# Score products of a head pair made together in a one-core encoder step

## The chip, the cores and the metric

The kernel runs on one core of one Trainium2 chip. The metric is device time in microseconds (us), from three timed runs of the whole program; lower is better. TensorE (PE in the profile) multiplies matrices, VectorE (DVE) and ScalarE (ACT) work elementwise, GpSimd (POOL) helps them, and SyncE (SP) issues the DMA transfers.

## The reference, cut to what matters

One step of a hybrid encoder layer is computed for 512 prompt tokens and 8 x 16 sample tokens, in float32. Two groups of heads read the same normalised input:

```python
oa = band_attend(qa..., band_gather(ka, 8), band_gather(va, 8), valid, bias=bias)   # 16 heads, width 64
ob = band_attend(qb..., band_gather(kb, 2), band_gather(vb, 2), valid, sink=sinks)  # 16 query heads, 2 key heads
...
s = einsum(q, k) * 64 ** -0.5        # scores; bias added, invalid keys masked
p = exp(s - max); w = p / sum(p)     # group B adds a sink to max and sum
o = einsum(w, v)
```

Then follow an output projection, a gated feed-forward network and a last norm. The change touches only the prompt tokens' score products, `einsum(q, k)`, and the order in which heads are worked on.

## The kernel before, in words

Tokens lie on the free axis (512 prompt columns and 128 sample columns), features on the 128 partitions. Every float32 product is made of three passes over parts of reduced precision, high x high, low x high and high x low: `mm3` at L147 to L149. The input projections are the main stream on TensorE: `dense` makes one tile of 128 output features from 16 input tiles, with two halves of 320 tokens, 96 matmuls of 128x320 in all. They are called "dense matmuls" below; in the profile they write `dn`.

Attention is side work. It is written as generators whose `yield`s cut them into stages. After every 6 dense matmuls (one input tile) `dense` calls `pump`, which emits one more stage; `get` also calls it as long as no on-chip slot is free, and the drains call it until a queue is empty. Two streams take turns at first, `heads 0` and `heads 1`, each with a head of its own. From the fifth round of projections on (`p == 4`) `heads 1` gives its place to `decode`, the attention of the sample tokens. After the eight rounds `drain_queue("decode")` emits what is left of it.

A 128-row tile of queries holds two heads of width 64, one in rows 0 to 63, the other in rows 64 to 127. `scores` multiplies one head's 64 rows: for a block `i` of 128 queries it fills one PSUM bank with 128 to 512 columns (group A) or 128 and 256 columns (group B), and a DVE instruction (L323) adds bias or mask and takes the row's maximum. There are four such blocks to a head, emitted two to a stage. `softmax` is an ACT exponential for each block (L332) and a DVE scaling (L339). Then `flip` transposes the weights on TensorE (L248), and their products with the values end the head.

The banks of side work come from a pool of four (`at`). The framework's scheduler may set an instruction before or after its neighbours, so the order that stands in the program is told from the built program where it matters.

The named stretch is this:

Of the kernel before, what the change touches and what calls it, by code (L numbers as in the profile page):

```python
# [8 lines left out]
ALU = mybir.AluOpType  # L9
# [4 lines left out]
P = 128  # L14
# [4 lines left out]
SP = 512  # L19
# [14 lines left out]
def active(step):  # L34
    """Pairs of ff tiles on chip in a step of the second half: each stays for eight steps."""
    return [j for j in range(NPAIR) if (step - START[j]) % STEPS < 8]
# [13 lines left out]
class Net:  # L50
    """Emission helpers over a fixed set of on-chip slots handed out in program order."""

    def __init__(self, nc, tc, io, pools):
        self.nc, self.tc, self.io, self.pools = nc, tc, io, pools
        self.uid = 0
        self.lists = {"S": [f"S{i}" for i in range(N_S)], "W": [f"W{i}" for i in range(N_W)]}
        self.owner, self.turns = {}, {}
        self.queues, self.active, self.turn = {}, {}, 0
        self.streams = (("heads 0", "heads"), ("heads 1", "heads"))

# [11 lines left out]
    def pump(self):  # L72
        """Emit one more stage of the side work; streams take turns."""
        for _ in range(len(self.streams)):
            name, queue = self.streams[self.turn % len(self.streams)]
            self.turn += 1
            work = self.active.get(name)
            if work is None and self.queues.get(queue):
                work = self.active[name] = self.queues[queue].pop(0)
            if work is None or work.gi_running:  # L80
                continue
            try:
                next(work)
            except StopIteration:
                self.active[name] = None
            return True
        return False
# [23 lines left out]
    def keep_turns(self):  # L111
        """A slot's tiles take it in program order."""
        first = {}
# [45 lines left out]
    def dense(self, chunks, acts, outs=1):  # L159
        """One tile of outputs, or several that share the passes over acts."""  # L160
        ps = [self.banks() for _ in range(outs)]
        k = 0
        for i in range(0, len(chunks), outs):
            now = [c if len(c) == 3 else self.weights(*c) for c in chunks[i:i + outs]]
            for j in range(now[0][0]):
                ah, al = acts[k]
                for (_, w, _), out in zip(now, ps):
                    for a in range(2):
                        t = slice(a * HT, a * HT + HT)
# [7 lines left out]
    def rstd_steps(self, parts, dim, out):  # L177
        """1 / sqrt(mean + eps) of the tokens of each half, in all partitions."""
        nc = self.nc
        ps, n = self.bank(), len(parts)  # L180
# [48 lines left out]
def build(nc, tc, io, pools):  # L229
# [33 lines left out]

# [1 line left out]
    n.move("S", "C", 7)  # L265
# [5 lines left out]

# [1 line left out]
    START_CHUNKS = {0: (24, 0, 2, "S"), 1: (25, 0, 2, "S"), 2: (24, 2, 8, "WH"), 4: (25, 2, 8, "WH"),  # L273
# [42 lines left out]

# [1 line left out]
    def scores(q, k, rr, i, k0, k1, bias, s, mx):  # L318
        ps = n.bank()[:, :k1 - k0]
        rows = slice(64 * rr, 64 * rr + 64)  # L320
        qs, ks = slice(128 * i, 128 * i + 128), slice(k0, k1)
        n.mm3(ps, (q[0][rows, qs], q[1][rows, qs]), (k[0][rows, ks], k[1][rows, ks]), True, True)
        nc.vector.tensor_tensor_reduce(s, ps, bias, 1.0, -3e38, ALU.add, ALU.max, mx)  # L323

# [28 lines left out]

    def prompt_a(h, q, k, v, ot, done):
        rr = h % 2
        bias, t0, t1 = n.get("S"), n.get("S"), n.get("S")
        dma(out=bias[:, :SP], in_=io["bias_a"][h])
        yield
        es = [t0[:, 512:640], t1[:, :256], t1[:, 256:640], t0[:, :512]]
        mx = n.small(4)  # L360
        for pick in ((0, 3), (1, 2)):
            for i in pick:
                scores(q, k, rr, i, 0, P * (i + 1), bias[:, SP - P * (i + 1):SP], es[i], mx[:, i:i + 1])
            yield
        softmax(es, mx, None)
        n.put("S", bias)
        yield
        yield
        yield
        yield  # L370
        blk = lambda i, j: es[i][:, P * j:P * j + P]
# [7 lines left out]
        o2, p2 = flip([blk(i, 2) for i in range(2, 4)], "S")  # L379
        n.put("S", t0, t1)  # L380
        yield
# [7 lines left out]

    def prompt_b(t, rr, q, ot, done):  # L390
        sink = sinks[:, 8 * rr + t:8 * rr + t + 1]
        t0, t1 = n.get("S"), n.get("S")
        es = [t0[:, 512:640], t0[:, :256], t0[:, 256:512], t1[:, :256]]
        mx = n.small(4)
        for pick in ((0, 1), (2, 3)):
            for i in pick:
                k0 = max(0, i - 1) * P
                w = (i + 1) * P - k0
                scores(q, kb, rr, i, k0, k0 + w, mask_b[:, 256 - w:], es[i], mx[:, i:i + 1])
            yield  # L400
        softmax(es, mx, sink)
        yield
        yield
        yield
        yield
        oa, pa = flip([es[0], es[1][:, :P], es[2][:, P:], es[3][:, :P]], "S")
        yield
        ob, pb = flip([es[1][:, P:], es[2][:, :P], es[3][:, P:]], "S")
        n.put("S", t0, t1)
        yield  # L410
# [11 lines left out]
    def heads_of(kind, p, held, *args):  # L422
# [10 lines left out]

        for rr in range(2):
            n.add("heads", kind(*((2 * p + rr,) if kind is prompt_a else (p, rr)), *args, ot, done))

# [170 lines left out]

# [1 line left out]
    n.add("heads", input_norm())  # L609
# [46 lines left out]
    for p in range(8):  # L656
# [3 lines left out]
        if p == 4:  # L660
# [3 lines left out]
            n.put("D", cos, sin)  # L664
            while n.active.get("heads 1"):
                n.pump()
            n.streams = (("heads 0", "heads"), ("decode", "decode"))
# [3 lines left out]

# [1 line left out]
    n.put("S", *xg, r_mix)  # L673
# [37 lines left out]

# [1 line left out]
    more = group_operands(oa_d, g_a, ssq_a, range(4, 8))  # L713
    own_a, acts_a = own_a + more[0], acts_a + more[1]

    def prepare(kts, in_place=()):
        """The seven left operands of pairs of feature tiles, one product at a time."""
        work = []
# [49 lines left out]

# [1 line left out]
    n.move("WH", "H", 4)  # L770
# [3 lines left out]
    def quartet(k, load, lefts, before=None, after=None, part="all"):  # L774
        """Weights b11, b12, b21, b22 against the seven left operands; yields each
        product's name and bank. The late part has the two products that only add
        to the first half of the tokens."""

# [130 lines left out]

# [1 line left out]
    sums, waiting = [], []  # L911
# [63 lines left out]

# [1 line left out]
    r_y = n.get("S")  # L977
# [131 lines left out]
```

## Time and profile before

| | |
|---|---|
| median of the three timed runs | 2725.25 us (2723.32 to 2726.64) |
| profiled execution: span from first to last instruction | 2722.2 us |
| median of the runs less that span (what lies around it) | 3.05 us |
| PE busy | 2645.7 us (97%) |
| DVE, ACT, POOL busy | 1933.8, 1063.8, 787.2 us |
| mean granted TensorE clock | 0.988 of full speed |

Matmuls overlap in the profile: each is busy for about 0.3 us while the next one starts after 0.15 us. So the time that a matmul costs is read from the start of one to the start of the next, and a stretch's pace from the number of matmuls that start in it.

### The profile page before, as it was taken

How to read it: one execution, taken by the hardware profiler on the slowest of the kernel's cores; microseconds unless marked ns; L12 is line 12 of the kernel's file. 1: busy time of each engine (PE TensorE's matmuls, PEld its weight loads, DVE VectorE, ACT ScalarE, POOL GpSimd, SP SyncE). 2: the span in 40 equal slices, each digit the busy share in tenths (PEclk: the TensorE clock that was granted, in tenths of full speed). 3: DMA queues.
4: the chain of work that ended last, by engine and by line, in shares of the span. 5: the costliest groups of instructions: out<-in, count | busy, mean ns of one | idle time of the engine just before them, and what ended most of it. 6: DMA issues, size and time to landing. Idle time of an engine off the chain costs nothing.

```text
span 2722.2 us, 45156 instructions
## 1 busy us (share of the span) xinstructions
PE 2645.7 (97%) x17757; PEld 2584.7 (95%) x17757; DVE 1933.8 (71%) x2947; ACT 1063.8 (39%) x1718; POOL 787.2 (29%) x564
## 2 busy tenths in 40 slices
PE   7999999999999999999999999999999899999986
PEld 7999999899899999999999999999999899999986
DVE  6555565655666678776767667667677878888897
ACT  4333333433544454333333333333334444444443
POOL 3000000000212123333343333333434533444453
PEclk9999999999899999999999999999999999999998
DMA  5222223333556443333232333332334644444334
GB/s 163 86 77 76 82 75 100 108 117 113 165 182 214 148 141 109 103 105 124 96 119 103 111 116 106 108 119 101 120 103 152 228 130 130 134 127 133 109 115 134
DMA packets 154149, 332.25 MB, mean 122 GB/s; under 512 B 18065, under 2 KB 69265, under 8 KB 153937
## 3 DMA queue, kind: packets, MB, share of 16 engines
q1 hardware_dynamic: 153936, 329.38, 36.9%
q8 instruction: 139, 2.28, 0.3%
q14 instruction: 74, 0.60, 0.1%
HBM read 274.38 MB, written 54.20 MB: 121 GB/s over the span
## 4 chain that ended last, share of the span: by engine, by line
PE 60%; DVE 5%; DMA 3%; issue 2%; ACT 1%; POOL 1%; SPq 0%; DVEq 0%; POOLq 0%; ACTq 0%
PE dn L149 12%; PE dn L147 12%; PE dn L148 12%; PE at L149 8%; PE at L148 8%; PE at L147 8%; DVE W L139 2%; DMA S<-act_d 1%; DVE S L828 1%; DMA W<-w_down 1%; DVE S L999 0%; DVE S L139 0%; DVE W L809 0%; DVE S L841 0%; POOL S L212 0%
## 5 line engine op out<-in xcount | busy, mean ns | idle before, releaser
L147 PE MATMUL dn<-S,W 128*128 128x320 f32 x3694 | 1164.8, 315 | 16.4 <-DVE S L828 6.3
L149 PE MATMUL dn<-S,W 128*128 128x320 f32 x3694 | 1150.5, 311 | 16.4 <-DVE W L139 16.4
L148 PE MATMUL dn<-S,W 128*128 128x320 f32 x3694 | 1148.9, 311 | 2.2 <-DVE S L143 1.1
L138 ACT ACTIVATE W<-W 128x1024 fp32r<-128x1024 f32 (+2 forms) x632 | 609.4, 965 | 1085.3 <-PE dn L148 551.4
L139 DVE TENSOR_TENSOR W<-W,W 128x1024 fp32r<-128x1024 f32 (+2 forms) x632 | 770.1, 1219 | 134.8 <-ACT W L138 130.2
L147 PEld LDWEIGHTS dn<-S,W 128*128 128x128 f32 x3694 | 699.5, 189 | 35.1 <-issue 17.3
L149 PEld LDWEIGHTS dn<-S,W 128*128 128x128 f32 x3694 | 699.4, 189 | 21.3 <-DVE W L139 21.0
L148 PEld LDWEIGHTS dn<-S,W 128*128 128x128 f32 x3694 | 700.0, 190 | 4.0 <-DVE S L143 1.4
L149 PE MATMUL at<-S,W 128*128 128x320 f32 (+2 forms) x1658 | 514.3, 310 | 7.5 <-DVE W L139 7.4
L147 PE MATMUL at<-S,W 128*128 128x320 f32 (+2 forms) x1658 | 513.6, 310 | 1.1 <-ACT W L138 1.1
L148 PE MATMUL at<-S,W 128*128 128x320 f32 (+2 forms) x1658 | 513.3, 310 | 0.2 <-DVE S L139 0.2
L811 POOL TENSOR_TENSOR W<-W,W 128x1024 f32<-128x1024 f32 (+2 forms) x76 | 162.8, 2142 | 587.0 <-DVE W L139 450.6
L149 PEld LDWEIGHTS at<-S,W 128*128 128x128 f32 x1658 | 311.3, 188 | 11.0 <-DVE W L139 10.3
L147 PEld LDWEIGHTS at<-S,W 128*128 128x128 f32 x1658 | 311.4, 188 | 1.6 <-ACT W L138 1.4
L148 PEld LDWEIGHTS at<-S,W 128*128 128x128 f32 x1658 | 311.3, 188 | 0.5 <-DVE S L139 0.5
L828 DVE TENSOR_TENSOR S<-S,dn 128x320 f32<-128x320 f32 x358 | 164.2, 482 | 104.0 <-PE dn L149 102.7
L807 DVE TENSOR_TENSOR W<-W,W 128x1024 f32<-128x1024 f32 (+2 forms) x76 | 140.2, 1845 | 89.4 <-DMA W<-w_up 46.6
L818 POOL TENSOR_TENSOR W<-W,W 128x1024 f32<-128x1024 f32 (+2 forms) x76 | 166.7, 2193 | 112.5 <-DVE W L139 107.0
L828 DVE TENSOR_TENSOR S<-S,at 128x320 f32<-128x320 f32 x262 | 123.5, 481 | 71.0 <-PE at L149 71.0
L212 POOL TENSOR_TENSOR S<-S,S 128x640 f32<-128x640 f32 x40 | 75.3, 1882 | 161.8 <-ACT S L211 161.4
L809 DVE TENSOR_TENSOR W<-W,W 128x1024 f32<-128x1024 f32 (+2 forms) x76 | 82.9, 1090 | 31.8 <-DMA W<-w_gate 23.0
L139 DVE TENSOR_TENSOR S<-at,S 128x512 fp32r<-128x512 f32 (+2 forms) x108 | 64.0, 604 | 53.0 <-ACT S L138 52.2
(141 smaller groups left out, 2306.6 us busy)
## 6 DMA issues: line engine op xcount, KB each, us to landing
W<-w_gate SPq DMA_DIRECT2D x88, 512.0 KB
W<-w_up SPq DMA_DIRECT2D x88, 512.0 KB
W<-w_in SPq DMA_DIRECT2D x66, 512.0 KB
W<-w_down SPq DMA_DIRECT2D x64, 384.0 KB
W<-w_down SPq DMA_DIRECT2D x68, 320.0 KB
act_d<-S SPq DMA_DIRECT2D x66, 320.0 KB
half<-act_d SPq DMA_DIRECT2D x81, 160.0 KB
S<-act_d SPq DMA_DIRECT2D x80, 160.0 KB
```

The lines of the kernel that those rows point to most:

```text
L138: self.nc.scalar.activation(hi, src, AF.Identity)
L139: self.nc.vector.tensor_tensor(lo, src, f(hi), ALU.subtract)
L147: mm(out, a[0], b[0], start=first, stop=False)
L148: mm(out, a[0], b[1], start=False, stop=False)
L149: mm(out, a[1], b[0], start=False, stop=last)
L212: (eng or nc.gpsimd).tensor_tensor(ssq, ssq, sq, ALU.add)
L807: nc.vector.tensor_tensor(b12[:, w], b12[:, w], b22[:, w], sub)
L809: nc.vector.tensor_tensor(s6[:, w], b11[:, w], b12[:, w], sub)
L811: nc.gpsimd.tensor_tensor(b11[:, w], b22[:, w], s6[:, w], sub)
L818: nc.gpsimd.tensor_tensor(b21[:, w], b21[:, w], s6[:, w], sub)
L828: add = lambda o, a, b: nc.vector.tensor_tensor(o, a, b, ALU.add)
```

## The change

`scores` now takes both heads of a tile. It takes two banks and issues the three passes in turn for rows 0 to 63 and rows 64 to 127, so that neighbours use the upper and the lower half of the array's rows. A generator works on a pair of heads: four score stages (one block of both heads each), two softmax stages, two empty stages, and then the rest of the two heads stage by stage in turn (`in_turn`). There is a single stream of pairs (joined by `decode` later). A pair of group A takes 16 pumps, where its two heads took 22; a pair of group B takes 15 in place of 20. The numbers of matmuls, DVE, ACT and DMA instructions of a pair stay.

```diff
-        self.streams = (("heads 0", "heads"), ("heads 1", "heads"))
+        self.streams = (("heads 0", "heads"),)
...
-    def scores(q, k, rr, i, k0, k1, bias, s, mx):
-        ps = n.bank()[:, :k1 - k0]
-        rows = slice(64 * rr, 64 * rr + 64)
+    def scores(q, k, i, k0, k1, biases, ss, mxs):
+
+        pss = [n.bank()[:, :k1 - k0] for _ in range(2)]
         qs, ks = slice(128 * i, 128 * i + 128), slice(k0, k1)
-        n.mm3(ps, (q[0][rows, qs], q[1][rows, qs]), (k[0][rows, ks], k[1][rows, ks]), True, True)
-        nc.vector.tensor_tensor_reduce(s, ps, bias, 1.0, -3e38, ALU.add, ALU.max, mx)
+        for x, (a, b) in enumerate(((0, 0), (0, 1), (1, 0))):
+            for rr, ps in enumerate(pss):
+                rows = slice(64 * rr, 64 * rr + 64)
+                nc.tensor.matmul(ps, q[a][rows, qs], k[b][rows, ks], start=x == 0, stop=x == 2)
+        for ps, bias, s, mx in zip(pss, biases, ss, mxs):
+            nc.vector.tensor_tensor_reduce(s, ps, bias, 1.0, -3e38, ALU.add, ALU.max, mx[:, i:i + 1])
+
+    def in_turn(works):
+
+        while works:
+            for w in list(works):
+                try:
+                    next(w)
+                    yield
+                except StopIteration:
+                    works.remove(w)
...
-        for pick in ((0, 3), (1, 2)):
-            for i in pick:
-                scores(q, k, rr, i, 0, P * (i + 1), bias[:, SP - P * (i + 1):SP], es[i], mx[:, i:i + 1])
-            yield
-        softmax(es, mx, None)
-        n.put("S", bias)
+        heads = []
+        for rr in range(2):
+            t0, t1 = n.get("S"), n.get("S")
+            heads.append(((t0, t1), [t0[:, 512:640], t1[:, :256], t1[:, 256:640], t0[:, :512]], n.small(4)))
+        for i in (3, 2, 1, 0):
+            w = P * (i + 1)
+            scores(q, k, i, 0, w, [x[:, SP - w:SP] for x in biases], [h[1][i] for h in heads], [h[2] for h in heads])
+            yield
+        n.put("S", *biases)
+        for _, es, mx in heads:
+            softmax(es, mx, None)
+            yield
         yield
         yield
-        yield
-        yield
+        yield from in_turn([tail_a(rr, own, es, v, ot, done) for rr, (own, es, _) in enumerate(heads)])
...
-        for pick in ((0, 1), (2, 3)):
-            for i in pick:
-                k0 = max(0, i - 1) * P
-                w = (i + 1) * P - k0
-                scores(q, kb, rr, i, k0, k0 + w, mask_b[:, 256 - w:], es[i], mx[:, i:i + 1])
-            yield
-        softmax(es, mx, sink)
+        for i in range(4):
+            k0 = max(0, i - 1) * P
+            w = (i + 1) * P - k0
+            scores(q, kb, i, k0, k0 + w, [mask_b[:, 256 - w:]] * 2, [h[1][i] for h in heads], [h[2] for h in heads])
+            yield
+        for rr, (_, es, mx) in enumerate(heads):
+            softmax(es, mx, sinks[:, 8 * rr + t:8 * rr + t + 1])
+            yield
...
-        for rr in range(2):
-            n.add("heads", kind(*((2 * p + rr,) if kind is prompt_a else (p, rr)), *args, ot, done))
+        n.add("heads", kind(p, *args, ot, done))
...
-            while n.active.get("heads 1"):
-                n.pump()
             n.streams = (("heads 0", "heads"), ("decode", "decode"))
```

`tail_a` and `tail_b` hold the old second halves of `prompt_a` and `prompt_b`, unchanged.

On TensorE, in the first round of projections, the first score stage of group A's first pair reads so before (`at_219` is the bank of block 0, `at_220` that of block 3, both of the head in rows 0 to 63; `W10` are the queries, `W11` the keys):

```order
L147 MATMUL at_219_1418<-W10_173_1080,W11_196_1259 128x128
L148 MATMUL at_219_1418<-W10_173_1080,W11_196_1259 128x128
L149 MATMUL at_219_1418<-W10_173_1080,W11_196_1259 128x128
L147 MATMUL at_220_1423<-W10_173_1080,W11_196_1259 128x512
L148 MATMUL at_220_1423<-W10_173_1080,W11_196_1259 128x512
L149 MATMUL at_220_1423<-W10_173_1080,W11_196_1259 128x512
```

At the same place the changed program has these (`at_220` is now block 3 of the upper head, `at_221` that of the lower one):

```order
L325 MATMUL at_220_1413<-W10_187_1143,W11_196_1259 128x512
L325 MATMUL at_221_1414<-W10_187_1143,W11_196_1259 128x512
L325 MATMUL at_220_1413<-W10_187_1143,W11_196_1259 128x512
L325 MATMUL at_221_1414<-W10_187_1143,W11_196_1259 128x512
L325 MATMUL at_220_1413<-W10_187_1143,W11_196_1259 128x512
L325 MATMUL at_221_1414<-W10_187_1143,W11_196_1259 128x512
```

The six matmuls of a stage now belong to two heads and one width. A pair of group A has four such stages with 6 dense matmuls between (12 from the fourth pair on); before, its two heads had two stages each, with the same distance. In group B the changed program has the four stages of a pair in one run of 24 matmuls (5 pairs) or two runs of 12 with 3 dense matmuls between (3 pairs); before, 6 pairs had four stages with 6 dense matmuls between, the first pair one run of 24, the second two runs of 12. Counted in the same way, the first transposes (L248) of the first eleven pairs stand 28 or 30 dense matmuls behind the last score matmul (37 for the very first), where 48 or 54 stood between before (35 for the first).

The other place is the end of the eight rounds of projections. There TensorE had before, a few dense matmuls into the output projection (`at_1266` are the transposed values of the last pair, `at_1275` scores of its first head, `at_1271` scores of the sample tokens):

```order
L147 MATMUL dn_1341_7807<-S37_1312_7742,W2_1343_7809 128x320
L248 MATMUL at_1266_7591<-cst_72,S7_1264_7586 128x128 x4
L147 MATMUL at_1275_7611<-W8_1174_7085,W9_1220_7336 128x128
L148 MATMUL at_1275_7611<-W8_1174_7085,W9_1220_7336 128x128
L149 MATMUL at_1275_7611<-W8_1174_7085,W9_1220_7336 128x128
L147 MATMUL at_1276_7616<-W8_1174_7085,W9_1220_7336 128x512
L148 MATMUL at_1276_7616<-W8_1174_7085,W9_1220_7336 128x512
L149 MATMUL at_1276_7616<-W8_1174_7085,W9_1220_7336 128x512
L147 MATMUL at_1271_7603<-S41_1272_7604,S15_920_5710 128x272
```

The changed program has there, with `at_1288` the transposed values and `at_1344` the pair's first scores 11 dense matmuls later:

```order
L147 MATMUL dn_1325_7752<-S50_1296_7687,W2_1327_7754 128x320
L248 MATMUL at_1288_7668<-cst_72,S7_1286_7663 128x128 x4
L148 MATMUL dn_1325_7752<-S20_1297_7688,W2_1327_7754 128x320
L149 MATMUL dn_1325_7752<-S50_1296_7687,W3_1328_7755 128x320
L147 MATMUL dn_1325_7752<-S50_1296_7687,W2_1327_7754 128x320
```

Before, 28 side matmuls stood here in one piece, and 28 and 24 more within the next 81 dense ones: what was left of `decode` and the scores of the last pair. In the changed program this part of `decode` has ended 98 dense matmuls earlier, and no more than 12 side matmuls stand together in that stretch.

## Rows read from the trace of the kernel before

**Rows 1.** The head of the page and its first part: span, then busy time of TensorE, share of the span and number of matmuls.

```profile
span 2722.2 us, 45156 instructions
PE 2645.7 (97%) x17757; PEld 2584.7 (95%) x17757; DVE 1933.8 (71%) x2947; ACT 1063.8 (39%) x1718; POOL 787.2 (29%) x564
```

**Rows 2.** Busy time by windows of 50 us, before and at the end of the rounds of projections: window and its length, then busy us and instructions (x) of PE, PEld, DVE, ACT and POOL, granted clock, DMA share, GB/s.

```profile
650.00:700.00 50.00, 50.00 (x334) 47.37 (x334) 28.38 (x71) 20.50 (x46) 1.92 (x9) 1.00 0.37 117
700.00:750.00 50.00, 47.82 (x270) 42.83 (x268) 36.69 (x80) 28.57 (x56) 16.57 (x20) 0.86 0.53 176
```

**Rows 3.** The timeline of TensorE, first score stage of group A's first head: start, duration, what.

```profile
146.27 0.31 PE L149 MATMUL dn<-S,W 128*128 128x320 f32 x1
146.51 0.33 PE L147 MATMUL at<-W,W 64*128 64x128 f32 x1
146.68 0.27 PE L148 MATMUL at<-W,W 64*128 64x128 f32 x1
146.79 0.28 PE L149 MATMUL at<-W,W 64*128 64x128 f32 x1
146.90 0.44 PE L147 MATMUL at<-W,W 64*128 64x512 f32 x1
147.18 0.39 PE L148 MATMUL at<-W,W 64*128 64x512 f32 x1
147.42 0.39 PE L149 MATMUL at<-W,W 64*128 64x512 f32 x1
147.74 0.41 PE L147 MATMUL dn<-S,W 128*128 128x320 f32 x1
147.99 0.31 PE L148 MATMUL dn<-S,W 128*128 128x320 f32 x1
```

**Rows 4.** The same of that head's second stage.

```profile
150.88 0.31 PE L149 MATMUL dn<-S,W 128*128 128x320 f32 x1
151.12 0.38 PE L147 MATMUL at<-W,W 64*128 64x256 f32 x1
151.34 0.28 PE L148 MATMUL at<-W,W 64*128 64x256 f32 x1
151.46 0.28 PE L149 MATMUL at<-W,W 64*128 64x256 f32 x1
...
151.93 0.34 PE L149 MATMUL at<-W,W 64*128 64x384 f32 x1
152.19 0.41 PE L147 MATMUL dn<-S,W 128*128 128x320 f32 x1
152.44 0.30 PE L148 MATMUL dn<-S,W 128*128 128x320 f32 x1
```

**Rows 5.** The timeline of TensorE around the two score stages of a head of group B: of each stage the last dense matmul before it and the second one behind it.

```profile
175.26 0.31 PE L149 MATMUL dn<-S,W 128*128 128x320 f32 x1
...
176.64 0.31 PE L148 MATMUL dn<-S,W 128*128 128x320 f32 x1
...
179.17 0.31 PE L149 MATMUL dn<-S,W 128*128 128x320 f32 x1
...
180.57 0.31 PE L148 MATMUL dn<-S,W 128*128 128x320 f32 x1
```

**Rows 6.** The same around the first pair of group B, whose 24 score matmuls stand in one run.

```profile
82.16 0.31 PE L149 MATMUL dn<-S,W 128*128 128x320 f32 x1
...
85.50 0.31 PE L148 MATMUL dn<-S,W 128*128 128x320 f32 x1
```

**Rows 7.** The timeline of TensorE in the second run of group B's second pair. In the program 12 matmuls stand here in the order L147, L148, L149 four times, the first six of rows 0 to 63, the other six of rows 64 to 127. A row marked x2 merges two neighbours of one line.

```profile
102.55 0.31 PE L149 MATMUL dn<-S,W 128*128 128x320 f32 x1
...
103.48 0.47 PE L147 MATMUL at<-S,S 64*128 64x256 f32 x2
103.60 0.28 PE L148 MATMUL at<-S,S 64*128 64x256 f32 x1
103.72 0.28 PE L149 MATMUL at<-S,S 64*128 64x256 f32 x1
103.80 0.28 PE L148 MATMUL at<-S,S 64*128 64x256 f32 x1
103.91 0.28 PE L149 MATMUL at<-S,S 64*128 64x256 f32 x1
...
104.72 0.31 PE L148 MATMUL dn<-S,W 128*128 128x320 f32 x1
```

**Rows 8.** The timeline of VectorE behind the run of rows 6: two neighbouring reductions of score blocks.

```profile
85.23 0.42 DVE L323 CUSTOM_DVE_ANT_0 S<-at,cst 128x256 f32<-128x256 f32 x1
...
85.58 0.42 DVE L323 CUSTOM_DVE_ANT_0 S<-at,cst 128x256 f32<-128x256 f32 x1
```

**Rows 9.** The timeline of VectorE in the softmax of the head of rows 3 and 4: its maxima negated, and its four scalings.

```profile
152.90 0.17 DVE L328 TENSOR_SCALAR sm<-sm 128x4 f32<-128x4 f32 x1
...
155.65 1.28 DVE L339 TENSOR_SCALAR S<-S,sm 128x128 f32<-128x128 f32 x4
```

**Rows 10.** The timeline of ScalarE behind the exponentials of that pair: one half of the split of a weight chunk.

```profile
157.50 1.05 ACT L138 ACTIVATE W<-W 128x1024 fp32r<-128x1024 f32 x1
```

**Rows 11.** The timeline of TensorE: the first transposes of that head.

```profile
162.36 0.60 PE L248 MATMUL at<-cst,S 128*128 128x128 f32 x4
```

More of the change, by code (lines that the diff above doesn't have):

```diff
@@ L352, in flip, with prompt_a, tail_a @@
         return own, hl
[L354 to L357, printed above, removed]
+    def prompt_a(p, q, k, v, ot, done):
+        biases = n.get("S"), n.get("S")
+        for rr, bias in enumerate(biases):
+            dma(out=bias[:, :SP], in_=io["bias_a"][2 * p + rr])
         yield
-        es = [t0[:, 512:640], t1[:, :256], t1[:, 256:640], t0[:, :512]]
-        mx = n.small(4)
-        for pick in ((0, 3), (1, 2)):
-            for i in pick:
-                scores(q, k, rr, i, 0, P * (i + 1), bias[:, SP - P * (i + 1):SP], es[i], mx[:, i:i + 1])
+        heads = []
[5 more added lines that the diff above has]
+            scores(q, k, i, 0, w, [x[:, SP - w:SP] for x in biases], [h[1][i] for h in heads], [h[2] for h in heads])
             yield
-        softmax(es, mx, None)
-        n.put("S", bias)
+        n.put("S", *biases)
+        for _, es, mx in heads:
+            softmax(es, mx, None)
+            yield
         yield
         yield
-        yield
-        yield
+        yield from in_turn([tail_a(rr, own, es, v, ot, done) for rr, (own, es, _) in enumerate(heads)])
+    def tail_a(rr, own, es, v, ot, done):
         blk = lambda i, j: es[i][:, P * j:P * j + P]
@@ L379, in prompt_a @@
         o2, p2 = flip([blk(i, 2) for i in range(2, 4)], "S")
-        n.put("S", t0, t1)
+        n.put("S", *own)
         yield
@@ L388, in prompt_a, with prompt_b, tail_b @@
         done()
[L390 to L394, printed above, removed]
-        for pick in ((0, 1), (2, 3)):
-            for i in pick:
-                k0 = max(0, i - 1) * P
-                w = (i + 1) * P - k0
-                scores(q, kb, rr, i, k0, k0 + w, mask_b[:, 256 - w:], es[i], mx[:, i:i + 1])
+    def prompt_b(t, q, ot, done):
+        heads = []
+        for rr in range(2):
+            t0, t1 = n.get("S"), n.get("S")
+            heads.append(((t0, t1), [t0[:, 512:640], t0[:, :256], t0[:, 256:512], t1[:, :256]], n.small(4)))
+        for i in range(4):
+            k0 = max(0, i - 1) * P
+            w = (i + 1) * P - k0
+            scores(q, kb, i, k0, k0 + w, [mask_b[:, 256 - w:]] * 2, [h[1][i] for h in heads], [h[2] for h in heads])
             yield
-        softmax(es, mx, sink)
+        for rr, (_, es, mx) in enumerate(heads):
+            softmax(es, mx, sinks[:, 8 * rr + t:8 * rr + t + 1])
+            yield
         yield
         yield
-        yield
-        yield
+        yield from in_turn([tail_b(rr, own, es, ot, done) for rr, (own, es, _) in enumerate(heads)])
+    def tail_b(rr, own, es, ot, done):
         oa, pa = flip([es[0], es[1][:, :P], es[2][:, P:], es[3][:, :P]], "S")
@@ L408, in prompt_b @@
         ob, pb = flip([es[1][:, P:], es[2][:, :P], es[3][:, P:]], "S")
-        n.put("S", t0, t1)
+        n.put("S", *own)
         yield
```

## The prediction

> **What bounds the kernel now.** I read the head of the page first: TensorE is busy for 2645.7 of 2722.2 us and VectorE for 71% of it [rows 1]. So the kernel is one long stream of matmuls, and a change is worth what it takes off that stream, or puts into it as idle time. The windows by 50 us give the stream's pace: 334 matmuls start in the window up to 700 us, which is 0.15 us for each, with the clock granted in full [rows 2]. The next window, the end of the projections, has 270 and a granted clock of 0.86: a place where the stream breaks. The timelines then show what a score stage costs, and whether the two halves of the array's rows can work at once.
>
> **What the score products cost now.** I take the time from the last dense matmul before a stage to the second one behind it, less the two steps of 0.15 us that would be there anyway. For the first stage of a head of group A that is 147.99 - 146.27 - 0.30 = 1.42 us [rows 3], for its second 152.44 - 150.88 - 0.30 = 1.26 us [rows 4]: 2.68 us a head, 5.36 us a pair, 42.9 us for eight pairs. For group B it is 1.08 + 1.10 = 2.18 us a head [rows 5], 4.36 us a pair for the six pairs that stand so. The first pair, already one run of 24 matmuls, costs 85.50 - 82.16 - 0.30 = 3.04 us [rows 6]. The second stands in two runs; the later costs 104.72 - 102.55 - 0.30 = 1.87 us [rows 7], and I take the earlier at the same, as an estimate: 3.74 us. Group B: 26.2 + 3.0 + 3.7 = 32.9 us. Both groups: 75.8 us, 2.8% of the span.
>
> **Do the two halves work at once?** In [rows 7] the program has one score product of the upper rows (L147, L148, L149) and then one of the lower rows. The trace shows L147 twice from 103.48, then L148, L149, L148, L149: the lower half's first matmul started ahead of the upper half's second. Each half goes on at its own 0.12 us (L148 to L149: 103.60 to 103.72, and 103.80 to 103.91), so neither slows the other. Five steps of 0.12 would be 0.60 us one after the other; they took 103.91 - 103.48 = 0.43 us. I read this as full overlap, without a price for sharing the array.
>
> The Trainium skill, "TensorE: Matmul & The Clock Gate", section "The mechanism", says that matmuls start and end strictly in program order, whatever rows they use. This case's trace does not agree: in [rows 7] a later matmul starts ahead of two earlier ones. By the rule, the 13 places where I count two neighbours of one half in the changed order of group B's runs would each lose about one step of 0.12 us, 1.6 us in all.
>
> **The change, part by part.** A stage now holds one width for both heads, and with full overlap lasts as long as one head's three matmuls. From the rows: into the stage 0.24 us; the first matmul, whose weights are not hidden, 0.17 us at 128 columns [rows 3] and 0.22 at 256 [rows 4]; the later ones 0.11, 0.12 and, at 512, 0.24; out of the stage 0.09 more than the last step and 0.25 to the second dense matmul. At 384 columns I put 0.28 and 0.18 between the neighbours, and 0.34 for the first at 512: estimates. So 128: 0.24 + 0.17 + 0.11 + 0.20 + 0.25 - 0.30 = 0.67; 256: 0.74; 384: 0.91; 512: 1.09. A pair of group A: 3.41 us, and some hundredths for the second half's later start, 3.45 in place of 5.36. Eight pairs save 15.3 us. The number of stages is the same, so what entering and leaving costs stays.
>
> In group B the four stages of a pair stand in one run, or nearly. Without other waits a run would take 0.67 us and three times about 0.41, 1.9 us in all. But it has eight score blocks and the pool has four banks: the third stage waits for the first one's reductions, the fourth for the second's. VectorE needs 85.58 - 85.23 = 0.35 us for one [rows 8]. They begin 0.55 us into the run, four end at 1.95, the last stage's matmuls then start up to 2.3 us: 0.24 + 2.3 + 0.21 + 0.25 - 0.30 = 2.7 us. Bounds: 1.9 us, and the 3.04 us of the run that exists [rows 6]. I take 2.7, since the reductions are the nearest rows. Eight pairs: 21.6 in place of 32.9, so 11.3 us saved (8.6 to 17.7).
>
> The Trainium skill, "TensorEngine Tiling (Array Packing)", section "PSUM Bottleneck", warns that packing speeds up the products and not the emptying of PSUM. By the rule group B's run is bound by VectorE; without it, 6.4 us more would be saved. Its reductions in [rows 8] follow each other without a gap, so the trace agrees.
>
> **The end of the projections.** A pair needs 16 or 15 pumps in place of 22 or 20, so `decode` gets more turns, and the pile of side work that `drain_queue("decode")` emits at the end is gone from the changed order. Before, the window there has 64 matmuls less than the one ahead of it: 64 x 0.15 = 9.6 us, part of it at the lower clock (0.86 over the window) [rows 2]. Loading and splitting the output projection's operands stays there. Bounds 0 and 9.6 us; I take 7, near the row, since a wait for the operands may stay.
>
> **What is lost.** With one stream a pair's softmax has less cover. For a head of group A the last score matmul starts at 151.93 [rows 4] and its four blocks are scaled at 155.65 + 1.28 = 156.93 [rows 9]: 5.0 us. Its transposes came at 162.36 [rows 11], so 5.4 us were to spare. In eleven pairs 28 or 30 dense matmuls now stand there: 30 x 0.15 + 0.25 for leaving the stage + three transposes of about 0.1 are 5.0 us until the last block is needed. That is just enough for the first head. The second head's exponentials follow the first's and its transposes come 6 dense matmuls later; and where the split of a weight chunk, 1.05 us on ScalarE [rows 10], falls between, TensorE waits for it. What is queued behind the transposes is the dense stream itself, which then stands still. Bounds: nothing, and one split and some tenths, 1.3 us, for each of eleven pairs, 14 us. I take 0.45 us each, 5 us. The later pairs alternate with `decode` and have 42 or more dense matmuls of cover or side work of `decode` between; they lose nothing. DVE, ACT and DMA do what they did, in less time; VectorE at 28 of 50 us [rows 2] has room.
>
> **The sum.** 2722.2 - 15.3 - 11.3 - 7 + 5 = 2693.6 us of span. The runs' median lies 3.05 us above the profiled span (2725.25 against 2722.2), so 2696.7: I predict 2697 us, 1.0% less. With the best ends of the terms it is 2725.25 - 15.3 - 17.7 - 9.6 = 2683; with the worst 2725.25 - 15.3 - 8.6 + 14 = 2715.
>
> **The rivals.**
> - *The halves do not overlap in this order.* Then a stage is six matmuls in a row: 1.0, 1.1, 1.45 and 1.8 us, 5.4 us a pair of group A, which saves nothing. Group B's runs cost 3.04 us each, 24.3 in place of 32.9. 2725.25 - 8.6 - 7 + 5 = 2715 us. Against it: [rows 7]. For it: only that alternation matmul by matmul has no row of its own. Chance 0.07.
> - *Softmax becomes the bound (slower).* The place is the first transposes of the eleven pairs. Their cover shrank by some 24 dense matmuls, 3.6 us. If head after head of softmax, with a weight chunk's halves in the queues of ScalarE and VectorE, took as long as the old distance, each pair would stop TensorE for 3.6 us: 11 x 3.6 = 40 us, and 2725.25 - 33.6 + 40 = 2732 us. It decides from 3.1 us a pair on. For it: a stop of some us also lowers the clock, as in the window of 0.86 [rows 2]. Against it: the 5.0 us of [rows 4, 9]. Chance 0.06.
> - *The gain is taken back.* TensorE comes earlier to the output projection and waits there for operands, which go through memory and are split by ScalarE and VectorE; and the 33.6 us become idle time. For it: that window is the one that already breaks [rows 2]. Against it: the scheduler has 98 dense matmuls without side work ahead of it to fetch them. Time: 2722 us. Chance 0.08.
> - *The forecast*, 0.79, with its own range of 2683 to 2715.
>
> A measurement here can tell 0.2% (5.5 us) from no change. Faster by more: the forecast and the first rival, 0.86. Within 0.2%: the third, 0.08. Slower: the second, 0.06. The forecast's own range holds the first rival's 2715 too and leaves out little more than the second and third, so the range is 2682 to 2716.
>
> **What would show it.** In the changed profile, score matmuls of equal line should start in twos, a hundredth or two apart, and a pair of group A should cost 3.4 to 3.5 us by the same count as above; runs of group B 2.5 to 3 us, with the third stage waiting for the reductions (L327 now). The window at the end of the projections should hold over 300 matmuls at a clock near 1. Idle time of TensorE ahead of L248 should be tenths of a us in each of the eleven pairs. The forecast is wrong if stages of one width last twice their three matmuls, if waits at L248 sum to over 14 us, or if the stream behind the projections starts earlier but the span doesn't end so.

## The result and the profile after

The changed kernel takes 2707.74 us (median of 4 runs, 2706.91 to 2710.12), the kernel before 2724.78 us beside it (2723.32 to 2726.64): a ratio of 0.9947, 95% interval 0.9935 to 0.996. That is 17 us less, where the prediction had 28 us less, 2697 us, with a range of 2682 to 2716. The profiled spans differ by nearly as much: 2706.5 and 2722.2 us.

The head of the page of the changed kernel, against [rows 1]:

```profile
span 2706.5 us, 45150 instructions
PE 2623.9 (97%) x17757; PEld 2566.7 (95%) x17757; DVE 1929.6 (71%) x2947; ACT 1063.5 (39%) x1718; POOL 788.1 (29%) x564
```

The number of matmuls is the same and TensorE is busy for 21.8 us less: time was saved inside the stream, and some of it is now idle time. The windows, against [rows 2] (columns as there):

```profile
650.00:700.00 50.00, 49.28 (x337) 46.73 (x336) 33.44 (x71) 26.68 (x55) 8.98 (x12) 1.00 0.41 133
700.00:750.00 50.00, 46.27 (x317) 43.85 (x316) 38.83 (x81) 26.55 (x52) 10.73 (x16) 0.97 0.56 182
```

The second window has 317 matmuls in place of 270 and a clock of 0.97 in place of 0.86. But TensorE is also idle in it for 3.7 us (50 less 46.27), where it was idle for 2.2 us before. Counted with half of the time at the lower clock, the window loses 5.4 us in place of 9.0: 3.7 us and half of 3.4 us now, 2.2 us and half of 13.6 us before. The timeline of TensorE shows the two kinds of score stage. First the stages of 512 and of 128 columns of a pair of group A, against [rows 3, 4] (start, duration, what; six matmuls of one line merge into one row):

```profile
144.83 0.30 PE L149 MATMUL dn<-S,W 128*128 128x320 f32 x1
145.06 0.96 PE L325 MATMUL at<-W,W 64*128 64x512 f32 x6
...
146.20 0.30 PE L148 MATMUL dn<-S,W 128*128 128x320 f32 x1
...
150.21 0.30 PE L149 MATMUL dn<-S,W 128*128 128x320 f32 x1
...
151.17 0.31 PE L148 MATMUL dn<-S,W 128*128 128x320 f32 x1
```

By the prediction's count the first costs 146.20 - 144.83 - 0.30 = 1.07 us (forecast 1.09) and the last 0.66 (forecast 0.67). The starts of the single matmuls come in twos, 1 to 6 ns apart. All four stages make 3.4 us a pair, forecast 3.45. Now two pairs of group B, against [rows 5, 6]. The first stands in two runs of 12, the second in one run of 24:

```profile
174.04 0.31 PE L147 MATMUL dn<-S,W 128*128 128x320 f32 x1
...
175.42 0.30 PE L149 MATMUL dn<-S,W 128*128 128x320 f32 x1
175.56 0.31 PE L147 MATMUL dn<-S,W 128*128 128x320 f32 x1
176.85 1.51 PE L325 MATMUL at<-S,S 64*128 64x256 f32 x12 [0.98 <-DVE sm L327]
...
178.54 0.31 PE L149 MATMUL dn<-S,W 128*128 128x320 f32 x1
...
200.78 0.31 PE L147 MATMUL dn<-S,W 128*128 128x320 f32 x1
201.01 2.73 PE L325 MATMUL at<-S,S 64*128 64x128 f32 x24
...
203.92 0.30 PE L149 MATMUL dn<-S,W 128*128 128x320 f32 x1
```

The run of 24 costs 203.92 - 200.78 - 0.30 = 2.84 us, near the forecast 2.7. The other pair costs 1.08 + 2.68 = 3.76 us: its second run waits 0.98 us for banks that the reductions (L327) have not yet read. VectorE began those late, behind the split of a weight chunk:

```profile
175.24 1.23 DVE L139 TENSOR_TENSOR W<-W,W 128x1024 fp32r<-128x1024 f32 x1 [0.99 <-PE at L325]
176.49 0.29 DVE L327 CUSTOM_DVE_ANT_0 S<-at,cst 128x128 f32<-128x128 f32 x1
```

Three of the eight pairs stand so. The two first ones, both in one run of 24, cost 2.94 and 4.28 us by the same count. The dear one waits for the split of its own queries (L138 and L139), and its end lies in a stretch at a granted clock of 0.50 (102.7 to 106.1 us) that the second trace of the changed kernel doesn't have; there it costs 3.78 us, with the same two waits:

```profile
99.89 0.72 PE L325 MATMUL at<-S,S 64*128 64x128 f32 x7 [0.29 <-ACT S L138]
100.96 2.55 PE L325 MATMUL at<-S,S 64*128 64x128 f32 x17 [0.34 <-DVE S L139]
```

All eight together take 27.0 us, where 21.6 were forecast; with group A's pairs all scores take 54.3 us.

Nearly all the idle time of the second window of 50 us is one stop. The timeline of TensorE, then of VectorE and of GpSimd ahead of it:

```profile
710.08 0.99 PE L248 MATMUL at<-cst,S 128*128 128x128 f32 x4 [3.73 <-DVE S L314]
```

```profile
693.98 0.88 DVE L143 SCALAR_TENSOR_TENSOR S<-S,cst,S 128x640 fp32r<-128x640 f32 x1
...
701.77 2.60 DVE L139 TENSOR_TENSOR W<-W,W 128x1024 fp32r<-128x1024 f32 x1
704.29 4.28 DVE L143 SCALAR_TENSOR_TENSOR S<-S,cst,S 128x640 fp32r<-128x640 f32 x2
...
709.20 0.82 DVE L314 TENSOR_TENSOR S<-dn,S 128x640 f32<-128x640 f32 x1
```

```profile
695.33 12.56 POOL L212 TENSOR_TENSOR S<-S,S 128x640 f32<-128x640 f32 x6 [3.79 <-ACT S L211]
```

TensorE waits for the last values tile, which VectorE scales at L314. That instruction stands behind splits of the output projection's operands (L143). A split takes 0.88 us at 693.98, but 4.28 / 2 = 2.14 us while GpSimd adds squares (L212), and a split of a weight chunk (L139) takes 2.60 us. Behind the stop the granted clock is at its lower level from 710.3 to 713.7 us.

### The profile page after: what moved, and what is told of

Read it like the earlier page. It is cut to its first block, busy times and chain, and to the rows that moved or that the text cites. A ratio compares the mean times of both kernels' runs of the same rounds, so it can differ in the third digit from the quotient of the medians.

```text
span 2706.5 us, 45150 instructions
## 1 busy us (share of the span) xinstructions
PE 2623.9 (97%) x17757; PEld 2566.7 (95%) x17757; DVE 1929.6 (71%) x2947; ACT 1063.5 (39%) x1718; POOL 788.1 (29%) x564
## 4 chain that ended last, share of the span: by engine, by line
PE 64%; DVE 5%; DMA 2%; issue 2%; ACT 0%; DVEq 0%; SPq 0%
PE dn L147 13%; PE dn L149 13%; PE dn L148 13%; PE at L149 8%; PE at L147 8%; PE at L148 8%; DVE W L139 2%; DVE S L846 1%; DMA S<-act_d 1%; DMA W<-w_down 1%; DVE S L1017 0%; PE at L619 0%; PE at L248 0%; DVE W L827 0%; DVE S L859 0%
## 5 line engine op out<-in xcount | busy, mean ns | idle before, releaser
L147 PE MATMUL dn<-S,W 128*128 128x320 f32 x3694 | 1162.4, 315 | 16.7 <-ACT S L858 6.6
L149 PE MATMUL dn<-S,W 128*128 128x320 f32 x3694 | 1153.0, 312 | 14.1 <-DVE W L139 14.0
L148 PE MATMUL dn<-S,W 128*128 128x320 f32 x3694 | 1153.3, 312 | 2.2 <-DVE S L143 1.1
L138 ACT ACTIVATE W<-W 128x1024 fp32r<-128x1024 f32 (+2 forms) x632 | 609.3, 965 | 1121.5 <-PE dn L148 558.3
L139 DVE TENSOR_TENSOR W<-W,W 128x1024 fp32r<-128x1024 f32 (+2 forms) x632 | 768.8, 1217 | 146.7 <-ACT W L138 139.6
L147 PEld LDWEIGHTS dn<-S,W 128*128 128x128 f32 x3694 | 701.0, 190 | 29.6 <-issue 10.2
L149 PEld LDWEIGHTS dn<-S,W 128*128 128x128 f32 x3694 | 701.0, 190 | 18.4 <-DVE W L139 17.9
L148 PEld LDWEIGHTS dn<-S,W 128*128 128x128 f32 x3694 | 701.1, 190 | 5.3 <-DVE S L143 1.4
L149 PE MATMUL at<-S,W 128*128 128x320 f32 (+3 forms) x1658 | 514.3, 310 | 6.3 <-DVE W L139 6.0
L147 PE MATMUL at<-S,W 128*128 128x320 f32 (+3 forms) x1658 | 513.7, 310 | 1.6 <-ACT W L138 1.6
L148 PE MATMUL at<-S,W 128*128 128x320 f32 (+3 forms) x1658 | 513.3, 310 | 0.0
L149 PEld LDWEIGHTS at<-S,W 128*128 128x128 f32 x1658 | 311.4, 188 | 9.8 <-DVE W L139 9.1
L147 PEld LDWEIGHTS at<-S,W 128*128 128x128 f32 x1658 | 311.5, 188 | 2.0 <-ACT W L138 1.9
L148 PEld LDWEIGHTS at<-S,W 128*128 128x128 f32 x1658 | 311.5, 188 | 0.0
L212 POOL TENSOR_TENSOR S<-S,S 128x640 f32<-128x640 f32 x40 | 76.0, 1899 | 166.4 <-ACT S L211 165.6
L138 ACT ACTIVATE S<-S 128x512 fp32r<-128x512 f32 (+2 forms) x90 | 54.7, 618 | 120.4 <-DVE S L645 31.9
```

The costliest lines, as they stand in the source:

```text
L138: self.nc.scalar.activation(hi, src, AF.Identity)
L139: self.nc.vector.tensor_tensor(lo, src, f(hi), ALU.subtract)
L147: mm(out, a[0], b[0], start=first, stop=False)
L148: mm(out, a[0], b[1], start=False, stop=False)
L149: mm(out, a[1], b[0], start=False, stop=last)
L212: (eng or nc.gpsimd).tensor_tensor(ssq, ssq, sq, ALU.add)
```

## The experiments

The expectations of the first four runs are in us of the chip on which the kernel before had taken 2724.8 us; on theirs it took 2720.9 us (13 runs). So I go by the ratios; 0.001 is 2.7 us. I also compare starts of the dense matmul that has 3840 others before it, called the 3840th here, which in these two kernels stands behind the last of the side work: 868.9 us in the trace of before, 851.3 us in that of the changed kernel.

**1. Do the halves overlap?** Here the second head's products also use rows 0 to 63, so they are not that head's; the number and the sizes of the matmuls stay.

```
-rows = slice(64 * rr, 64 * rr + 64)
+rows = slice(0, 64)
```

> Both heads of a pair are multiplied from rows 0 to 63, so the second head's scores are those of the first; all else is the changed kernel. Theory (the gain is the overlap of the two halves): a stage of group A becomes six matmuls in a row, 1.0, 1.1, 1.45 and 1.8 us for 128 to 512 columns where the changed kernel shows 0.68, 0.74, 0.92 and 1.09; about 16 us more in group A and 3 to 6 us in group B, so 2727 to 2730 us, no better than before. Rival (the gain comes from the single stream and its fewer pumps): 2708 to 2713 us.

Measured: ratio 1.003 (1.002 to 1.0041), span 2725.7 us. The whole gain is gone, and 0.3% more than that, which was not taken apart. Its timeline has the stage of 512 columns and a run of 24:

```profile
147.21 0.31 PE L149 MATMUL dn<-S,W 128*128 128x320 f32 x1
147.45 1.65 PE L325 MATMUL at<-W,W 64*128 64x512 f32 x6
...
149.29 0.31 PE L148 MATMUL dn<-S,W 128*128 128x320 f32 x1
```

```profile
205.10 0.31 PE L147 MATMUL dn<-S,W 128*128 128x320 f32 x1
...
208.69 0.31 PE L149 MATMUL dn<-S,W 128*128 128x320 f32 x1
```

The stage costs 1.78 us against 1.07, so what the change saves in group A is overlap. The run of 24 costs 208.69 - 205.10 - 0.30 = 3.29 us against 2.84: in group B overlap is worth no more than 0.45 us in such a pair. That fits a pace that the reductions set and not TensorE; this run does not show it by itself.

**2. Is it the alternation?** Three passes of the upper head, then three of the lower:

```
-for x, (a, b) in enumerate(((0, 0), (0, 1), (1, 0))):
-    for rr, ps in enumerate(pss):
-        rows = slice(64 * rr, 64 * rr + 64)
+for rr, ps in enumerate(pss):
+    rows = slice(64 * rr, 64 * rr + 64)
+    for x, (a, b) in enumerate(((0, 0), (0, 1), (1, 0))):
```

> The three passes of the upper head stand ahead of the three of the lower one, all else is the changed kernel. Theory (each half of the rows takes its next matmul as soon as it is free, ahead of matmuls of the other half that stand earlier): the lower half starts one to two steps after the upper, a stage costs 0.1 to 0.15 us more, 2711 to 2714 us. Rival (matmuls start strictly in program order): the lower half's first waits for the upper half's third, two steps more per stage, 0.24 us at 256 columns and 0.47 at 512, 12 to 16 us in all, 2720 to 2724 us.

Measured: 0.9962 (0.9949 to 0.9977), span 2708.9 us. The stage of 512 columns:

```profile
144.49 0.30 PE L149 MATMUL dn<-S,W 128*128 128x320 f32 x1
144.72 0.97 PE L325 MATMUL at<-W,W 64*128 64x512 f32 x6
...
145.88 0.31 PE L148 MATMUL dn<-S,W 128*128 128x320 f32 x1
```

It costs 1.09 us, as with alternation. In group A's stages of this program three of one half stand in front of the other half's first. In the trace the starts still come in twos, now some 10 ns apart, so that first one did not wait for the three. That rules out the rival; and the 0.1 us more that the theory put on a stage is not there either. The change earns its gain by having both heads in one stage; the order inside is worth nothing that was measured.

**3. What does group B's early start cost?** A pair of group B takes fewer stages than there are in a tile's time, so it begins right when it is added, and its products pile up until its queries are through `rope` and split. The edit puts 13 empty stages ahead of it.

```
 def prompt_b(t, q, ot, done):
+    for _ in range(13):
+        yield
```

> A pair of group B begins with 13 empty stages, so that its queries have been turned by the rotary steps when its scores are emitted. Theory (group B's runs of 12 and 24 pile up because a pair now begins before its queries are there, and the second run of 12 waits 1.0 us for reductions): four stages of 6 with dense matmuls between, 2.9 us a pair in place of 2.85, 3.78 or 4.29, 4 us less, and up to 3 us less of waits ahead of transposes and value products: 2701 to 2704 us. Rival (the piles cost nothing that spacing gives back, or the later pairs push side work to the end): 2707 us or more.

Measured: 0.9945 (0.9932 to 0.9958), 2710 us on the chip of the expectations: by its total this is the rival's, and it can't be told from the changed kernel's 0.9947. But the trace shows what the theory expected. The four stages of a pair now stand apart; the first two:

```profile
178.82 0.31 PE L149 MATMUL dn<-S,W 128*128 128x320 f32 x1
...
179.79 0.30 PE L148 MATMUL dn<-S,W 128*128 128x320 f32 x1
...
180.37 0.31 PE L149 MATMUL dn<-S,W 128*128 128x320 f32 x1
...
181.42 0.31 PE L148 MATMUL dn<-S,W 128*128 128x320 f32 x1
```

They cost 0.67 and 0.75 us, the pair 2.92. No wait for L327 is left. So four separate stages cost about as much as one run of 24 (2.84 us): what the run saves at its ends it loses to the reductions. By the count above all scores take 50.7 us in place of 54.3, but the 3840th dense matmul starts only 2.0 us earlier.

**4. What is the stop ahead of L248?** The squares on VectorE in place of GpSimd:

```
-n.add_square(ssq, o, t == 0, "S")
+n.add_square(ssq, o, t == 0, "S", nc.vector)
```

> The sums of squares of the output projection's operands are added on VectorE in place of GpSimd, in both groups. Theory (TensorE's stop of 3.9 us at the end of the projections comes from operand splits on VectorE that take 2.2 us in place of 0.88 while GpSimd adds): the splits take 0.9 us, the stop falls below 1.5 us, 2703 to 2705 us. Rival (VectorE's queue is simply too long there, 7 additions more make it longer): the stop stays or grows, 2708 to 2712 us.

Measured: 0.9932 (0.992 to 0.9945). The window of 700 to 750 us, and a split with a square behind it on VectorE:

```profile
700.00:750.00 50.00, 48.90 (x344) 46.32 (x343) 38.26 (x88) 28.60 (x56) 3.75 (x15) 1.00 0.61 202
```

```profile
703.67 0.88 DVE L143 SCALAR_TENSOR_TENSOR S<-S,cst,S 128x640 fp32r<-128x640 f32 x1
704.47 0.82 DVE L212 TENSOR_TENSOR S<-S,S 128x640 f32<-128x640 f32 x1
```

Every split takes 0.88 us again. VectorE does 0.82 us more work for each operand, and is through with both in less time than with the split alone before. The stop and the lower clock are gone, 344 matmuls start in place of 317, and the 3840th dense matmul starts 5.6 us earlier.

**5. The two together,** with the changed kernel once more on the same chip (the kernel before took 2721.5 us there).

> The changed kernel once more, without an edit, so that the next three have it beside them on the same chip. Both theories: 0.994 to 0.995 of the kernel before, and TensorE stands 3.7 us ahead of L248 near 706 us.

> The 13 empty stages ahead of a pair of group B and the squares on VectorE, together. Theory (each edit is worth what its own place in the trace shows: 2.0 us at the end of the side work for the empty stages, 4.1 us ahead of L248 near 706 us for the squares; the rest of the two spans' differences lay in stretches at the lower clock that have nothing to do with them): 5 to 8 us below the changed kernel on the same chip, ratio to the kernel before 0.9915 to 0.993. Rival (the spans' differences of 6.3 and 7.3 us are all due to the edits): 13 to 14 us below, ratio 0.9895. Second rival (the two share a wait): 4 us below or less.

The changed kernel again: 2708.74 us, 0.9963 (0.9951 to 0.9976), and the stop of 3.7 us is there. Both edits: 2696.92 us, 0.9912 (0.9899 to 0.9925), 11.8 us below it by medians. That is between theory and rival. By the trace the 3840th dense matmul starts 7.1 us earlier, near the 7.6 us of runs 3 and 4 (2.0 + 5.6); the spans differ by 8.8 us.

**6. Does decode wait because its stages stand closer?** In the changed kernel the transposes of decode wait for ScalarE and VectorE where they did not before. Here decode takes only every second turn.

```
-def pump(self):
+def pump(self, idle=False):
...
     if work is None or work.gi_running:
+        if idle:
+            return True
         continue
...
-self.pump()
+self.pump(True)
```

(the last in `dense` alone)

> Between the dense matmuls decode takes only every second turn, also while no pair of heads has work; what is left of it is made at the end, before the output projection. Theory (in the changed kernel decode's stages stand 6 dense matmuls apart instead of 12 as soon as a pair is done, so its transposes wait for ScalarE and VectorE): the idle time of TensorE ahead of L248, without the one stop of 3.7 us, falls from 2.0 us between 440 and 700 us to under 0.8 us, and the dense matmul 3168 starts 4 to 6 us earlier (also because less of decode stands before it); the pile at the end gives that back, so the total is within 4 us of the changed kernel on the same chip. Rival (the waits come from the load of ScalarE and VectorE and not from the distance of the stages): the idle time ahead of L248 stays at 2 us or more.

Measured: 1.0028 (1.0019 to 1.0038), 18 us above the changed kernel by the ratios, 21 us by the medians. TensorE's waits, engine and line waited for, us in total, times, longest, from 440 to 700 us; L250 here is L248 in the changed kernel:

```profile
...
PE at L250 <- ACT S L592: 0.7, 1, 0.7
PE at L250 <- DVE S L518: 0.7, 1, 0.7
PE at L250 <- DVE S L519: 0.3, 1, 0.3
```

The same stretch of the changed kernel has 0.9, 0.2 and 0.9 us for these three sources (L590, L516, L517). The waits did not go: the distance is not shown to be their cause. And the pile of decode work at the end is dear. The window of 900 to 950 us here, and the longest wait of TensorE from 850 to 1100 us:

```profile
900.00:950.00 50.00, 46.22 (x281) 44.65 (x282) 35.65 (x50) 28.26 (x44) 14.61 (x8) 0.88 0.39 132
```

```profile
PE dn L149 <- ACT S L144: 5.0, 1, 5.0
```

In the second run of the changed kernel 343 matmuls start in that window, at a clock of 1.00. The pile delays the operands of the projection behind it (L144 makes one half of their split, behind their load), and TensorE stops for them. The 3168th dense matmul starts 13 us earlier, as less of decode stands before it, but the total is far outside the 4 us that I had expected.

**7. Is softmax's cover just enough?** The two empty stages behind a pair's softmax are left out in both groups.

```
     yield
-    yield
-    yield
     yield from in_turn(...)
```

> Without the two empty stages behind the softmax of a pair: the first transposes of a pair of group A then stand 23 dense matmuls behind its last score product instead of 30. Theory (the cover is just enough, as the prediction counted: 5.0 us needed and 5.0 us there): 7 x 0.15 = 1.05 us of idle time ahead of L248 in each of some ten pairs, so 8 to 12 us slower than the changed kernel on the same chip. Rival (the cover had slack, as the near absence of such waits in the changed kernel's trace lets one think): within 3 us, and idle time ahead of L248 under 0.3 us a pair.

Measured: 0.998 (0.9972 to 0.9989), 4.6 us above the changed kernel by the ratios, in the profiles 12 us by the 3840th dense matmul; the profiled execution, of 2720.3 us, was one of the two longest of eleven. But the transposes hardly wait: L248 lists 1.3 us of idle time for L353 in 130 to 440 us. The price came at another place, the products of group B:

```profile
197.19 0.31 PE L149 MATMUL dn<-S,W 128*128 128x320 f32 x1
198.12 0.44 PE L325 MATMUL at<-S,S 64*128 64x128 f32 x4 [0.62 <-ACT S L138]
198.85 0.73 PE L325 MATMUL at<-S,S 64*128 64x128 f32 x8 [0.29 <-DVE S L139]
...
200.66 1.90 PE L325 MATMUL at<-S,S 64*128 64x256 f32 x12 [0.45 <-DVE sm L327]
```

With two stages less, a pair reaches its products before its queries are split, and TensorE stops for the split itself, as it does in the changed kernel for group B's second pair. From 200.4 to 207.2 us the granted clock is 0.50. So the theory falls in its mechanism: softmax had slack, and the two empty stages pay by keeping group B back, as the 13 stages of run 3 do further.

**8. Is the stop new?** The edit of run 4 in the kernel before, and the three other variants once more, on one chip (the kernel before: 2721.9 us).

> The kernel before, with the squares of the output projection's operands on VectorE (the one edit of ops_dve). Theory (the stop of 3.7 us ahead of L248 is one that the change itself made: in the kernel before only two or so of the eight operand splits took over 2 us and no such stop is there): within 2 us of the kernel before, ratio 0.999 to 1.0005. Rival (squares on GpSimd cost the kernel before as much as the changed one): 4 to 7 us faster, ratio 0.9975 to 0.9985.

> Once more the squares on VectorE alone, on one chip with the two runs that follow. Theory (an edit is worth what its own place in the trace shows): ratio to the kernel before some 0.0015 to 0.002 below that of the changed kernel, so 0.993 to 0.9945. Rival (worth 7 us): 0.9925 or less.

> Once more the 13 empty stages alone. Theory: 2 us, so a ratio some 0.001 below that of the changed kernel, 0.994 to 0.9955. Rival (worth 6 us): 0.9935 or less.

> Once more both edits. Theory (the two add up, 2.0 and 5 us): a ratio 0.0025 to 0.003 below that of the changed kernel, 0.992 to 0.993. Rival (together they are worth more than the two alone, as the first run's median of 11.8 us below the changed kernel lets one think): 0.9915 or less, while the two alone stay above 0.993.

The kernel before with squares on VectorE: 0.9988 (0.9979 to 0.9997), 3.3 us faster by the ratio, span 2715.5 us, and its 3840th dense matmul starts 6.0 us earlier. The ratio lies between theory and rival, and its interval reaches into both. So the kernel before seems to pay for these squares too; how, the two traces don't show. Without the edit TensorE stops for 0.86 us ahead of L599, in front of 10.2 us at the lower clock, and with it neither is there. But nothing in the traces ties that stop to the squares. First the trace without the edit, then with it:

```profile
715.50:725.70 10.20, 10.20 (x37) 8.76 (x36) 7.52 (x17) 5.56 (x10) 4.26 (x4) 0.50 0.51 164
710.62 0.83 ACT L142 ACTIVATE S<-S,cst 128x640 fp32r<-128x640 f32 x1 [1.75 <-DMA S<-ob_d]
712.29 0.74 DVE L595 TENSOR_SCALAR S<-at,sm 128x512 f32<-128x512 f32 x1
713.09 1.08 PE L599 MATMUL at<-cst,S 128*128 128x32 f32 x8 [0.86 <-DVE S L595]
```

```profile
700.00:750.00 50.00, 48.18 (x308) 42.79 (x308) 42.66 (x102) 31.13 (x60) 5.70 (x17) 1.00 0.58 185
710.61 0.83 ACT L142 ACTIVATE S<-S,cst 128x640 fp32r<-128x640 f32 x1 [0.87 <-DMA S<-ob_d]
712.28 0.74 DVE L595 TENSOR_SCALAR S<-at,sm 128x512 f32<-128x512 f32 x1
713.07 1.08 PE L599 MATMUL at<-cst,S 128*128 128x32 f32 x8
```

The awaited L595 comes at the same time in both. It stands on VectorE behind the split of an operand (L143), that waits for ScalarE's half (L142), and that for the operand's load. TensorE comes to L599 0.86 us later with the edit, and 0.66 us of this delay are there at the dense matmul with 300 before it (73.29 against 72.63 us), far ahead of the first square at 704.1 us. So the stop went because TensorE came later. Of the lower clock behind it the cause stays open.

The repetitions: squares alone 0.993 (0.9917 to 0.9944), empty stages alone 0.9945 (0.9933 to 0.9958), both 0.9912 (0.9899 to 0.9926). With the changed kernel at 0.9947 and 0.9963, measured apart from these three, the squares are worth some 0.0024 (6.6 us), the empty stages 0.001 (2.7 us, not clear of noise) and both 0.0043 (11.7 us). Within their intervals they add up. The version with both, 2697 us, is faster than the changed kernel and the kernel before.

## Why the prediction was right, and where it was not

- **The two halves overlap:** right, and shown by run 1. Reading it off one stretch of before [rows 7] was enough. The rule of program order that was weighed there does not hold here: in run 2 it would have kept the second head's first matmul behind three others, and the stage cost the same.
- **Group A, 15.3 us:** right. 3.4 us a pair against the forecast 3.45; 5.36 before.
- **Group B, 11.3 us:** the first step that failed by size. The runs of 24 were sized rightly (2.84 against 2.7 us), but the sum took all eight pairs as such runs. Three stand in two runs of 12 with a wait of 0.98 us, and one pair waits for its queries. 27.0 us in place of 21.6; against the forecast 32.9 before, 5.9 us saved. The prediction saw that the reductions bound a run, and didn't ask when a pair starts and whether VectorE is free then; run 3 takes the runs apart and the waits go.
- **The end of the projections, 7 us:** the second step that failed by size. The prediction expected the lower clock and the idle time of [rows 2] to go with the pile, and counted only on a wait for operands that may stay. By the windows of 700 to 750 us 3.6 us came (9.0 less 5.4). What is missing lies in the new stop of 3.73 us with 3.4 us at the lower clock behind it, and run 4 shows where that stop comes from: operand splits that take 2.14 us beside GpSimd's squares in place of 0.88. The prediction put no price on these. With the squares on VectorE the window of the changed kernel loses 1.1 us, which would have been 7.9 us saved against the kernel before. Whether the pile made the loss before is not shown, though: in run 8's trace the kernel before keeps its pile and loses 1.8 us there (50 less 48.18, at a clock of 1.00). The 64 matmuls that the prediction counted as lost were not all lost time either; that window has 308 and not 334 at the full clock.
- **Softmax, 5 us lost:** too much. In the changed kernel no wait at L248 is listed between 106 and 440 us, in the profile's view of waits for TensorE; this is all that it lists:

```profile
PE at L325 <- DVE sm L327: 2.9, 3, 1.0
```

- **The sum.** 15.3 + 5.9 + 3.6 = 24.8 us by the terms as measured; 17.6 us are there at the 3840th dense matmul. Of the 7.2 us between, 3.0 us are more waits from 440 to 700 us (4.0 us in all against 1.0), 2.0 of them ahead of decode's transposes (0.9 + 0.9 + 0.2); their cause stays open. The stretch at the lower clock from 102.7 to 106.1 us costs half its length, 1.7 us. The rest, and the 1.9 us that the span loses behind that point, were not taken apart; the changed kernel's trace has two more short stretches at the lower clock there, at 2222 and 2588 us, with nothing of the change near. None of this is in the prediction. That its time is off by 11 us and not by more is luck in part: the 5 us that it put down for softmax did not come, and that makes up for 5 of the some 9 us (7.2 + 1.9) that it had left out.
- **The rivals.** "The gain is taken back" named the right place: TensorE stops at the output projection, for a values tile that is queued behind the operands' splits. But the price was 5.6 us and not 33.6. "Softmax becomes the bound" did not come; run 7 shows that with less cover it is the queries of group B that are late first.

## What to carry to other kernels

Products that use half of the array's rows belong in one stage with those of the other half; how the two are ordered inside it did not matter here. Where a run of such products needs more banks than there are, count the reductions and ask when each run can start: separate stages cost about as much as the run. Before a slow window is put down to the work that a change removes, look which instructions in it are slower than elsewhere, on every engine that runs beside them. And where a stop is gone after an edit, see whether the awaited instruction came earlier or TensorE came later.

## What the runs showed of the hardware

- Matmuls of the two row halves go on independently even when three of one half stand in the program ahead of the other's first: 1.09 us for the stage in that order, 1.07 us in alternation, 1.78 us when all six use one half.
- While GpSimd adds two SBUF tiles of 128x640, VectorE's split of such a tile takes 2.14 us in place of 0.88, and a weight split 2.60 in place of 1.22. The Trainium skill, "SBUF — State Buffer", section "Who interferes with whom", says that a VectorE instruction with two inputs in SBUF contends with a GpSimd instruction that reads SBUF. The trace agrees, and the prediction had not counted it.
- Short stops stood in front of longer stretches at the lower clock: 0.86 us in the kernel before ahead of 10.2 us at 0.50, and 0.62, 0.29 and 0.45 us in run 7 ahead of 6.8 us at 0.50. At half the clock these stretches cost about half their length, more than the stops. Not every stop has such a stretch behind it: the three waits of 0.98 us in group B have none, and the waits of 0.29 and 0.34 us in group B's second pair have 3.4 us in one trace of the changed kernel and none in the other.
